# Other orders of the products in a projection block, in the experts and in the second MLP

## The chip, the cores and the metric

The kernel runs on one core of one Trainium2 chip, in one launch, and its time is the device time of that core in microseconds (us). Five engines work side by side, each through its own list of instructions: PE (TensorE, matmuls, with its weight loads shown apart as PEld), DVE (VectorE), ACT (ScalarE), POOL (GpSimd) and SP (SyncE, which here only issues DMAs). They meet through semaphores.

## The reference

Two transformer blocks are applied to 256 tokens of 1024 features. The first block (`first_block`) is a gated branch mixer, cross attention to 256 memory tokens and a two-level mixture of experts; the second (`second_block`) runs two layers with an adaLN modulation each: sparse attention with an MLP, then differential attention with an MLP. Cut to what the change touches:

```python
proj = h @ w_in                                   # 1024 -> 6 widths, and 3 gates of 1024
...
return merged @ w_o
...
k, v = jnp.split(mem_n @ w_xkv, 2, axis=-1)       # mem_n: the memory behind its own norm
...
act = silu(einsum('nd,edf->nef', t, w_e_gate)) * einsum('nd,edf->nef', t, w_e_up)
out = einsum('nef,efd->nd', act * gate, w_e_down) # 16 experts of 256 features
```

All of it is fp32. The sums over the inner dimension may be taken in any order.

## The kernel before

**Three products for one.** Each fp32 operand is split into a high and a low part (`whi`, `wlo` for weights; `hTh`, `hTl` and the like for activations), and a product is high·high + high·low + low·high. Weights come by DMA into `raw`, 512 KB at a time; ACT copies them to `whi` (line L98) and DVE subtracts for `wlo` (L99). `raw`, `whi` and `wlo` have six buffers each. PE then multiplies: `mm_fm` (L140 to L142) with the weights as the stationary operand and 256 tokens as the moving one, `mm_tm` (L147 to L149) with 128 tokens stationary and 512 weight columns moving.

**Blocks.** `fm_block` makes 256 output features in one bank of PSUM, 128 features (f = 0, 1) in each half of it. With an inner dimension of 1024 there are 8 row blocks k, so 2·8·3 = 48 matmuls. A block whose input is still being made (`first=True`, and `out_first`) goes over k outside and f inside; every other block takes f outside and k inside, three products for each. The mixer's `proj`, the keys of the memory (`fm<-memT`), the heads of the cross attention, the output projections (`out_proj`), the gates and the upper halves of both MLPs (`fm<-hT`) are such blocks.

**The memory's path.** `norm_rows` normalises the memory's two tiles of 128 tokens: squares on ACT (L247), then `rv`, `r` (L253, an Exp) and `memx` on DVE (L257). `to_fm` turns them on PE (L338, sixteen transposes in four groups, `ax`), copies them to `memTh` on ACT (L341) and takes `memTl` on DVE (L342). Around it ACT has a sine and a cosine (L591, L592) and two kinds of sigmoids (L637 for the conv branch, `sg`; L642 for the condition, `sgc`), each of which needs another function table than the Exp; a load of a table is `ACT_TABLE_LOAD`. DVE makes the condition (`cond`, L643) from `sgc`.

**Experts.** Each of the 16 experts, four to a group (gi), takes `gu` (8 k by 3 products), then `py` = hidden · w_e_down: for k, for the two halves n, three products, into two banks of PSUM. Behind a group's fourth expert its two banks are split to `yh` (L215, ACT) and `yl` (L216, DVE), and `po` (L1080) sums the group into the residual. Behind the last group come the sums of squares (`ss`, L1092 and L1126) of the next norm.

**The second MLP.** `down` (`mo`, `mm_fm`) goes over k, f and three products, into the halves of four banks.

**Who sets the order.** The program text is not the order of the instructions. A scheduler of the framework simulates the engines and puts each engine's list in the order in which its simulation would start the instructions; dependences and a few fences (`behind`) are all that the text fixes.

Of the kernel before, what the change touches and what calls it, by code (L numbers as in the profile page):

```python
# [19 lines left out]
P = 128  # L20
S = 256
# [17 lines left out]
def two_blocks_kernel(ctx, tc, A, out):  # L39
# [10 lines left out]
    # PSUM's eight banks, shared out anew for each phase: outputs of long runs of matmuls (mm), what hangs  # L50
    # on a chain of other engines (ax), long accumulations (acc), modulation rows (ada)
# [24 lines left out]
    # ---------------------------------------------------------------- helpers  # L76
# [28 lines left out]
    class wmat:  # L105
        """the hi and lo parts of w2d[:, c0:c0+cols], as [128, cols] pairs, one for each 128 rows"""
# [30 lines left out]
    def mm_fm(ps, w, x, xk, c, first, last, ncol=P, **kw):  # L137
        """ps[ncol features, tokens] += w[:, c:c+ncol]^T x[:, xk, :]"""
# [5 lines left out]
    def mm_tm(ps, xT, xk, t0, w, first, last):  # L144
        """ps[128 tokens, cols] += x[:, xk, t0:t0+128]^T w"""
# [4 lines left out]

    def fm_block(w2d, K, c0, x, w=None, first=False):
# [16 lines left out]
    def tm_steps(w2d, c0, xT, emit, cols=512, w=None):  # L168
        """512 output columns for both token tiles, a tile at a time"""
# [33 lines left out]
    def skewed(gens, fill=None):  # L203
        """software pipeline: each round starts a generator and moves the others on by one step, newest first"""
# [20 lines left out]
    def inv_rms(ss, n, scale, tag, pool=None):  # L225
        """1/sqrt(ss * scale + EPS) for ss [128, n], with one Newton step on top of the tables' exp(-ln / 2)"""
# [5 lines left out]
    def newton(ss, y, h, t, scale, add=EPS, p=P):  # L232
        """y = 1/sqrt(ss * scale + add)"""
# [7 lines left out]
    def norm_rows(x, dst):  # L241
        """dst = x / rms(x), for x [128 tokens, 1024]"""
# [20 lines left out]
    def rstd(ss, add=EPS):  # L263
        """1/rms of the tokens from their sums of squares on all partitions"""
# [4 lines left out]
    class norm:  # L269
        """the norm of x times gA plus gB, as hi and lo"""  # L270
# [6 lines left out]
        def squares(self, c):  # L277
            """features 256c on of x: their squares' sums over partitions; those of the first 768 are added up before"""
# [39 lines left out]
    def resid(c, ps, gate=None, nx=None):  # L318
        """features 256c on: x += gate * ps, and what the next norm takes from them"""
# [11 lines left out]
    def to_fm(h, aT, t, g):  # L331
        """rows [128 tokens, 1024] times gains to hi/lo feature-major columns of token tile t"""
# [12 lines left out]
    def out_first(aT, w, k1, k0=0, ps=None):  # L345
        """the first block of out_proj up to row block k1, for an input that is still under way"""
# [7 lines left out]
    def out_proj(aT, w2d, nx, gate=None, ws=(), ps0=None):  # L354
        """x += gate * (a @ w)"""
# [9 lines left out]
    # ---------------------------------------------------------------- constants  # L365
# [10 lines left out]
    # the residual stream, feature-major  # L376
# [7 lines left out]
    # causal mask of a diagonal block, twice  # L384
# [6 lines left out]
    # ---------------------------------------------------------------- adaLN rows  # L391
# [3 lines left out]
    def cols(n, name, *parts):  # L395
        """vectors as columns: rows of 128 values turned, [128, n]"""
# [14 lines left out]
    # a part of a layer's modulation row at a time, 1024 columns, in steps of 128 rows of w_ada: on TensorE, 256 for  # L411
    # each of its four column tiles, or summed up over steps on VectorE
# [22 lines left out]
    def ada_mm(n=1, pool=None):  # L435
        """steps on TensorE, or with a pool for the sum on VectorE"""
# [47 lines left out]
    def adaln(i, j, g):  # L484
        """columns of (1 + scale) * g and shift of sublayer j"""
# [10 lines left out]
    # ================================================================ block 1  # L496
    with tc.tile_pool(name="kv", bufs=1, reuse_waits="tile") as kvp:
# [15 lines left out]
        # ---- gated branch mixer  # L513
        win = A["w_in"][0]
        log_exp()
        with tc.tile_pool(name="mix", bufs=1, reuse_waits="tile") as mx:
# [17 lines left out]
            def turned(src, name, c):  # L534
                """features 256c on of two tiles of rows, feature-major"""
# [18 lines left out]
            # the memory's norm, for its keys and values  # L554
# [10 lines left out]
            # rope tables, [128 tokens, tile, 8]  # L565
# [48 lines left out]
            # conv branch  # L614
# [30 lines left out]
            # gated short conv branch  # L645
# [20 lines left out]
            # pool branch  # L666
# [20 lines left out]
            # layer norm over the conv channels  # L687
# [29 lines left out]
            # gates 1 and 2 with their branches  # L717
# [114 lines left out]
            # logits, feature-major, then turned  # L832
# [11 lines left out]
    # ---- hierarchical mixture of experts  # L844
# [7 lines left out]
    def head_rstd(pool, src, n, dim, tag):  # L852
        """1/rms over the last axis of src [128, n, dim]"""
# [6 lines left out]
    def head_norm(pool, dst, src, n, gain, tag):  # L860
        """dst [128, n, 64] = rms_norm(src) * gain, for src in PSUM"""
# [4 lines left out]
    def rope(pool, dst, src, t, n):  # L866
        """the first 16 of 64 columns of dst [128, n, 64] rotated; dst may be src"""
# [834 lines left out]
```

## Time and profile before

| | before |
|---|---|
| median of three runs | 1259.2 us (1256.54 to 1259.34) |
| span of the profiled execution | 1263.1 us |
| PE busy | 1214.8 us, 96% |
| DVE busy | 891.7 us, 71% |
| ACT busy | 695.9 us, 55% |
| mean granted TensorE clock | 0.974 |
| read from HBM | 255.15 MB |

The profile is one execution of its own, whose span is the time from its first to its last instruction; it is 0.3% longer than the median. "Busy" is the time in which an engine has at least one instruction under way. A matmul's end is modelled, so the pace of a dense stretch is read from the distance between starts. The granted clock is a share of 2.4 GHz.

### The profile page before, as it was taken

The page shows a single profiled execution, that of the slowest core. Times are in us where ns is not written, and L with a number is a line of the kernel's source. Part 1 is how long each engine was busy: PE and PEld are TensorE (multiplying, and loading weights), DVE is VectorE, ACT ScalarE, POOL GpSimd, SP SyncE. Part 2 cuts the span into 40 slices and gives each one's busy share as a digit, 9 for nine tenths or more (in the row PEclk, how much of TensorE's full clock was granted, in tenths as well). Part 3 has the DMA queues.
Part 4 walks back from the last instruction along what each step waited for, and adds up shares of the span by engine and source line. Part 5 has one row for each costly group of instructions (what it writes and reads, how often), then busy time and mean ns, then how long its engine had stood idle before and what let it go on. Part 6 is the DMA issues. An engine that isn't in the chain of part 4 may idle for free.

```text
span 1263.1 us, 22514 instructions
## 1 busy us (share of the span) xinstructions
PE 1214.8 (96%) x8762; PEld 1079.8 (85%) x8762; DVE 891.7 (71%) x1672; ACT 695.9 (55%) x1163; POOL 26.0 (2%) x33
## 2 busy tenths in 40 slices
PE   7999999999879999899999989999999999999998
PEld 6989999989667888688656879999988767999998
DVE  7999967564568999696756685486679766645453
ACT  6644447453357777566346465455556554655453
POOL 0000000000000000060000000000000000000000
PEclk8999999999889999999769999999999999999999
DMA  7565565791267999665431697586746445555551
GB/s 247 190 220 174 159 205 186 269 305 37 97 219 259 347 354 345 231 205 169 149 110 58 213 345 267 192 302 221 281 167 207 130 134 201 196 196 179 194 172 34
DMA packets 177551, 257.76 MB, mean 204 GB/s; under 512 B 14239, under 2 KB 138999, under 8 KB 177436
## 3 DMA queue, kind: packets, MB, share of 16 engines
q1 hardware_dynamic: 177436, 256.24, 61.1%
q8 instruction: 71, 1.16, 0.4%
q14 instruction: 44, 0.36, 0.1%
HBM read 255.15 MB, written 1.05 MB: 203 GB/s over the span
## 4 chain that ended last, share of the span: by engine, by line
PE 65%; DVE 3%; DMA 2%; ACT 1%; issue 1%; ACTq 0%; DVEq 0%
PE fm L141 6%; PE fm L142 6%; PE fm L140 6%; PE mo L140 5%; PE mo L141 5%; PE mo L142 5%; PE tm L147 3%; PE tm L149 3%; PE tm L148 3%; PE gu L149 2%; PE gu L147 2%; PE gu L148 2%; PE s L1393 2%; PE ada L432 1%; PE py L148 1%; PE py L149 1%
## 5 line engine op out<-in xcount | busy, mean ns | idle before, releaser
L99 DVE TENSOR_TENSOR wlo<-raw,whi 128x1024 fp32r<-128x1024 f32 (+1 forms) x382 | 456.8, 1218 | 178.0 <-ACT whi L98 173.9
L98 ACT ACTIVATE whi<-raw 128x1024 fp32r<-128x1024 f32 (+1 forms) x382 | 391.6, 1048 | 275.4 <-PE fm L141 149.3
L141 PE MATMUL fm<-hTl,whi 128*128 128x256 f32 (+1 forms) x968 | 276.7, 286 | 5.6 <-DVE hTl L216 3.9
L140 PE MATMUL fm<-hTh,whi 128*128 128x256 f32 (+1 forms) x968 | 276.3, 286 | 3.2 <-ACT hTh L215 3.2
L142 PE MATMUL fm<-hTh,wlo 128*128 128x256 f32 (+1 forms) x968 | 275.0, 284 | 0.0
L141 PEld LDWEIGHTS fm<-hTl,whi 128*128 128x128 f32 (+1 forms) x968 | 185.8, 192 | 7.7 <-DVE hTl L216 5.8
L140 PEld LDWEIGHTS fm<-hTh,whi 128*128 128x128 f32 (+1 forms) x968 | 185.8, 192 | 5.7 <-ACT hTh L215 4.6
L142 PEld LDWEIGHTS fm<-hTh,wlo 128*128 128x128 f32 (+1 forms) x968 | 185.7, 192 | 0.2
L141 PE MATMUL mo<-ul,whi 128*128 128x256 f32 x512 | 142.8, 280 | 0.0
L142 PE MATMUL mo<-uh,wlo 128*128 128x256 f32 x512 | 142.7, 280 | 0.0
L140 PE MATMUL mo<-uh,whi 128*128 128x256 f32 x512 | 141.7, 281 | 0.0
L141 PEld LDWEIGHTS mo<-ul,whi 128*128 128x128 f32 x512 | 96.3, 188 | 0.0
L142 PEld LDWEIGHTS mo<-uh,wlo 128*128 128x128 f32 x512 | 96.2, 188 | 0.0
L140 PEld LDWEIGHTS mo<-uh,whi 128*128 128x128 f32 x512 | 95.5, 188 | 0.4 <-issue 0.4
L147 PE MATMUL tm<-whi,hTh 128*128 128x512 f32 x176 | 69.4, 400 | 0.7 <-ACT hTh L215 0.7
L148 PE MATMUL tm<-wlo,hTh 128*128 128x512 f32 x176 | 68.9, 393 | 0.0
L149 PE MATMUL tm<-whi,hTl 128*128 128x512 f32 x176 | 68.1, 392 | 0.0
L141 PE MATMUL fm<-oTl,whi 128*128 128x256 f32 x192 | 55.0, 289 | 0.9 <-DVE oTl L1613 0.8
L140 PE MATMUL fm<-oTh,whi 128*128 128x256 f32 x192 | 53.9, 288 | 1.4 <-ACT oTh L1612 1.3
L142 PE MATMUL fm<-oTh,wlo 128*128 128x256 f32 x192 | 53.6, 283 | 0.0
L147 PE MATMUL gu<-whi,xgh 128*128 128x512 f32 x128 | 51.1, 401 | 1.8 <-ACT xgh L1011 1.8
L627 DVE SCALAR_TENSOR_TENSOR acv<-apad,chv,acv 128x256 f32<-128x256 f32 x120 | 51.3, 475 | 0.0
(522 smaller groups left out, 2163.1 us busy)
## 6 DMA issues: line engine op xcount, KB each, us to landing
ada<-in_w_ada_dram SPq DMA_DIRECT2D x96, 512.0 KB, 4.7
raw<-in_w_mlp_in_dram SPq DMA_DIRECT2D x64, 512.0 KB, 3.8
raw<-in_w_mlp_out_dram SPq DMA_DIRECT2D x64, 512.0 KB, 5.1
raw<-in_w_in_dram SPq DMA_DIRECT2D x48, 512.0 KB, 3.8
raw<-in_w_e_down_dram SPq DMA_DIRECT2D x32, 512.0 KB, 5.2
raw<-in_w_e_gate_dram SPq DMA_DIRECT2D x61, 256.0 KB, 5.0
raw<-in_w_e_up_dram SPq DMA_DIRECT2D x61, 256.0 KB
raw<-in_diff_w_in_dram SPq DMA_DIRECT2D x24, 512.0 KB, 4.1
```

The lines of the kernel that those rows point to most:

```text
L98: behind("A", SC.activation(hi[:, :n], raw[:, :n], AF.Copy))
L99: last["lo"] = behind("V", V.tensor_tensor(lo[:, :n], raw[:, :n], hi[:, :n].bitcast(F32), op=OP.subtract))
L140: T.matmul(ps, whi[:, c:c + ncol], xh[:, xk, :], start=first, stop=False, **kw)
L141: T.matmul(ps, whi[:, c:c + ncol], xl[:, xk, :], start=False, stop=False, **kw)
L142: return T.matmul(ps, wlo[:, c:c + ncol], xh[:, xk, :], start=False, stop=last, **kw)
L147: T.matmul(ps, xh[:, xk, t0:t0 + P], w[0], start=first, stop=False)
L148: T.matmul(ps, xh[:, xk, t0:t0 + P], w[1], start=False, stop=False)
L149: return T.matmul(ps, xl[:, xk, t0:t0 + P], w[0], start=False, stop=last)
L432: behind("T", T.matmul(ada_part["ps"][32 * j:32 * j + 32, :], w, r[:, S * j:S * j + S], start=start, stop=stop, skip_group_check=True))
L627: V.scalar_tensor_tensor(acv[:, f, :], apad[:, f, j:j + S], chv[:, f, j:j + 1], acv[:, f, :], op0=OP.mult, op1=OP.add)
L1393: T.matmul(ss[hp][:, :n], u, k[:, gi, 0:t + 1].rearrange("p a s q -> p (a s q)"), start=k is kTd, stop=False)
```

## The change

Every block of `fm_block` but the first ones now takes one of five orders, by turns of a counter. `by_rows` has k outside, then f, then the three products. `by_parts` has k, then the product, then f, so that the half written changes with each matmul. `by_features` has f, k and the products as high·low, high·high, low·high. `by_rows_turned` is `by_parts` with the two halves swapped in the middle product. `by_runs` has f, then the product, then k. Odd experts, and the lower products of the groups 2 and 3, use `mm_tm2`, which takes the low part of the tokens first and the low part of the weights last; the pairs (k, n) of `py` come in two other sequences. In the second MLP (i = 1) `down` has k, product, f. No product is added or removed, and no DMA, tile or buffer is changed; comments are taken out, which moves the line numbers.

```diff
+    def by_rows(ps, w, x, K):
+        for k in range(K):
+            for f in range(2):
+                fence["T"] = mm_fm(ps[:, f * S:(f + 1) * S], w[k], x, k, f * P, k + f == 0, k + f == K,
+                                   skip_group_check=True)
...
+    def by_parts(ps, w, x, K):
+        for k in range(K):
+            for j in range(3):
+                for f in range(2):
+                    a, b = parts(w, x, k, f)[j]
+                    fence["T"] = T.matmul(ps[:, f * S:(f + 1) * S], a, b, start=k + j + f == 0, stop=k + j + f == K + 2,
+                                          skip_group_check=True)
...
+    orders = (by_rows, by_parts, by_features, by_rows_turned, by_runs)
...
-            for f in range(2):
-                for k in range(K):
-                    fence["T"] = mm_fm(ps[:, f * S:(f + 1) * S], w[k], x, k, f * P, k == 0, k == K - 1)
+            orders[turn["fm"] % len(orders)](ps, w, x, K)
+            turn["fm"] += 1
...
+    def mm_tm2(ps, xT, xk, t0, w, first, last):
+
+        xh, xl = xT
+        T.matmul(ps, xl[:, xk, t0:t0 + P], w[0], start=first, stop=False)
+        T.matmul(ps, xh[:, xk, t0:t0 + P], w[0], start=False, stop=False)
+        return T.matmul(ps, xh[:, xk, t0:t0 + P], w[1], start=False, stop=last)
...
-                            for f in range(2):
-                                # one group for the bank: its first product clears both halves
+                            for n, f in ((n, f) for n in range(3) for f in range(2)) if i == 1 else ():
+                                a, b = parts([tuple(v[:, 2 * c * P:] for v in wk) for wk in (w[0], w[1])], u, k, f)[n]
+                                T.matmul(po[c][:, f * S:(f + 1) * S], a, b, start=j + k + n + f == 0,
+                                         stop=j + k + n + f == 19, skip_group_check=True)
```

The scheduler places the other engines' work anew around the new order of the products. Two places show it. The first is the memory's path, 28 to 53 us into the run. On ACT, before, both `r` stand together, then the sine's table, the cosine, the sigmoid's table and the condition's sigmoid:

```order
L253 ACTIVATE r_265<-rv_256 128x1
L253 ACTIVATE r_309<-rv_300 128x1
L591 ACT_TABLE_LOAD
L591 ACTIVATE sin_367<-ang_351 128x16
L592 ACTIVATE cos_368<-kk_360 128x16
L642 ACT_TABLE_LOAD
L642 ACTIVATE sgc_1107<-col0_117 128x8
L98 ACTIVATE whi_645<-raw_643 128x1024
L98 ACTIVATE whi_651<-raw_649 128x1024
L637 ACTIVATE sg_499<-fm_450 128x512
L341 ACTIVATE memTh_251<-ax_271,gcols_249 128x128
```

The same place of ACT now (`whi_645` stands two rows above the first, and `whi_721` and `memTh_251` follow the last):

```order
L305 ACTIVATE r_265<-rv_256 128x1
L98 ACTIVATE whi_651<-raw_649 128x1024
L689 ACT_TABLE_LOAD
L689 ACTIVATE sg_499<-fm_450 128x512
L305 ACT_TABLE_LOAD
L305 ACTIVATE r_309<-rv_300 128x1
L643 ACT_TABLE_LOAD
L643 ACTIVATE sin_367<-ang_351 128x16
L644 ACTIVATE cos_368<-kk_360 128x16
L694 ACT_TABLE_LOAD
L694 ACTIVATE sgc_1107<-col0_117 128x8
L98 ACTIVATE whi_715<-raw_713 128x1024
```

The conv branch's sigmoid and a weight copy now stand between the two `r`, there are two table loads more, and two weight copies more come ahead of `memTh`. On PE, before, the first twelve transposes of the memory stand in the third `proj` block (`fm_518`), at matmul 149 of the program:

```order
L141 MATMUL fm_518<-hTl_166,whi_514 128x256
L142 MATMUL fm_518<-hTh_165,wlo_515 128x256
L338 MATMUL ax_271<-ident_78,memx_253 128x128 x4
L338 MATMUL ax_284<-ident_78,memx_253 128x128 x4
L338 MATMUL ax_315<-ident_78,memx_297 128x128 x4
L140 MATMUL fm_518<-hTh_165,whi_514 128x256
L141 MATMUL fm_518<-hTl_166,whi_514 128x256
```

Now they stand in the fourth (`fm_583`, by `by_rows_turned`), from matmul 190 on:

```order
L170 MATMUL fm_583<-hTl_166,whi_573 128x256 x2
L170 MATMUL fm_583<-hTh_165,wlo_574 128x256
L390 MATMUL ax_271<-ident_78,memx_253 128x128 x4
L390 MATMUL ax_284<-ident_78,memx_253 128x128 x4
L170 MATMUL fm_583<-hTh_165,wlo_574 128x256
L170 MATMUL fm_583<-hTh_165,whi_573 128x256
L390 MATMUL ax_315<-ident_78,memx_297 128x128 x4
L170 MATMUL fm_583<-hTh_165,whi_573 128x256
```

They moved 41 matmuls later. The last four transposes (`ax_328`, row blocks 4 to 7 of the second token tile) moved from matmul 228, ahead of the first product with the memory (248), to 282, behind 43 of these products (from 239 on). The low part of row block 7 (`memTl`) is first used at matmul 371 instead of 314, that of row block 6 at 348 instead of 305.

The second place is the end of the expert layer. On PE, before, the last expert's `py` ends with both halves side by side, n = 0 (`py_7325`) two matmuls ahead of n = 1 (`py_7326`):

```order
L147 MATMUL py_7325<-whi_7491,eah_7455 128x512
L147 MATMUL py_7326<-whi_7491,eah_7455 128x512
L148 MATMUL py_7325<-wlo_7492,eah_7455 128x512
L149 MATMUL py_7325<-whi_7491,eal_7456 128x512
L148 MATMUL py_7326<-wlo_7492,eah_7455 128x512
L149 MATMUL py_7326<-whi_7491,eal_7456 128x512
L1080 MATMUL po_7513<-PT_5938,yh_7507 128x256
```

Now n = 0 ends last:

```order
L200 MATMUL py_7326<-whi_7491,eal_7456 128x512
L201 MATMUL py_7326<-whi_7491,eah_7455 128x512
L200 MATMUL py_7325<-whi_7491,eal_7456 128x512
L201 MATMUL py_7325<-whi_7491,eah_7455 128x512
L202 MATMUL py_7326<-wlo_7492,eah_7455 128x512
L202 MATMUL py_7325<-wlo_7492,eah_7455 128x512
L1135 MATMUL po_7513<-PT_5938,yh_7507 128x256
```

On ACT, before, the two halves of `yh` stand together, ahead of a weight copy for the next layer:

```order
L98 ACTIVATE whi_7558<-raw_7556 128x1024
L215 ACTIVATE yh_7507<-py_7325 128x512
L215 ACTIVATE yh_7507<-py_7326 128x512
L98 ACTIVATE whi_7564<-raw_7562 128x1024
L1089 ACTIVATE sq_7519<-xT_88 128x512 x4
```

Now the copy stands between them, and n = 0, which the first `po` reads, comes second:

```order
L98 ACTIVATE whi_7558<-raw_7556 128x1024
L267 ACTIVATE yh_7507<-py_7326 128x512
L98 ACTIVATE whi_7564<-raw_7562 128x1024
L267 ACTIVATE yh_7507<-py_7325 128x512
L1144 ACTIVATE sq_7519<-xT_88 128x512 x4
```

DVE follows: `wlo_7565` (L99) now stands between the two halves of `yl`. On PE all eight sums of squares of the next norm stand behind the last `po`, where two of them stood between the third and the fourth before.

## Rows read from the trace of the kernel before

**Rows 1.** The page, busy time and instructions of each engine.

```profile
PE 1214.8 (96%) x8762; PEld 1079.8 (85%) x8762; DVE 891.7 (71%) x1672; ACT 695.9 (55%) x1163; POOL 26.0 (2%) x33
```

**Rows 2.** The first stretch of 100 us: length, busy us of PE, PEld, DVE, ACT, POOL; PEclk, DMA, GB/s.

```profile
0.00:100.00 100.00, 89.41 (x618) 83.61 (x619) 88.92 (x208) 57.17 (x97) 1.28 (x11) 0.97 0.68 219
```

**Rows 3.** Idle time of PE by what ended it: total us, times, longest.

```profile
PE ax L338 <- issue: 1.8, 1, 1.8
```

**Rows 4.** Starts on PE in dense stretches: start us, us, engine, line, operation.

```profile
718.75 0.28 PE L140 MATMUL fm<-oTh,whi 128*128 128x256 f32 x1
...
719.35 0.28 PE L142 MATMUL fm<-oTh,wlo 128*128 128x256 f32 x1
...
1178.07 0.28 PE L142 MATMUL mo<-uh,wlo 128*128 128x256 f32 x1
...
1179.01 0.28 PE L141 MATMUL mo<-ul,whi 128*128 128x256 f32 x1
```

**Rows 5.** Groups by shape on PE: us busy, mean ns of one | idle.

```profile
L148 PE MATMUL gu<-wlo,xgh 128*128 128x512 f32 x128 | 50.8, 398 | 0.0
...
L148 PE MATMUL py<-wlo,eah 128*128 128x512 f32 x64 | 25.6, 405 | 0.5 <-DVE wlo L99 0.5
```

**Rows 6.** ACT in order of time, 28 to 35 us.

```profile
27.93 1.06 ACT L98 ACTIVATE whi<-raw 128x1024 fp32r<-128x1024 f32 x1 [0.99 <-PE fm L141]
...
29.08 0.33 ACT L253 ACTIVATE r<-rv 128x1 f32<-128x1 f32 x2
...
30.84 0.20 ACT L592 ACTIVATE cos<-kk 128x16 f32<-128x16 f32 x1
31.05 1.28 ACT L642 ACT_TABLE_LOAD   x1
32.34 0.21 ACT L642 ACTIVATE sgc<-col 128x8 f32<-128x8 f32 x1
32.46 1.99 ACT L98 ACTIVATE whi<-raw 128x1024 fp32r<-128x1024 f32 x2
...
34.83 0.35 ACT L341 ACTIVATE memTh<-ax,gcols 128x128 fp32r<-128x128 f32 x1
```

**Rows 7.** DVE in order of time, 32 to 57 us.

```profile
32.58 0.17 DVE L643 TENSOR_TENSOR cond<-col,sgc 128x8 f32<-128x8 f32 x1 [2.08 <-ACT sgc L642]
...
32.86 1.68 DVE L257 TENSOR_SCALAR memx<-memx,r 128x512 f32<-128x512 f32 x4
...
52.57 0.34 DVE L342 SCALAR_TENSOR_TENSOR memTl<-ax,gcols,memTh 128x128 fp32r<-128x128 f32 x1
52.83 4.43 DVE L627 SCALAR_TENSOR_TENSOR acv<-apad,chv,acv 128x256 f32<-128x256 f32 x11
```

**Rows 8.** DMA issues, 14 to 50 us: KB each, median us from issue to landing.

```profile
raw<-in_w_xkv_dram SPq DMA_DIRECT2D x12, 512.0 KB, 4.5
```

**Rows 9.** SyncE's DMA issues in order of time, 28 to 47 us.

```profile
28.33 17.16 SPq L92 DMA_DIRECT2D raw<-in_w_xkv_dram  x10
```

**Rows 10.** PE in order of time, 33 to 35 us and 45 us.

```profile
33.45 1.50 PE L338 MATMUL ax<-ident,memx 128*128 128x128 f32 x12 [1.83 <-issue]
...
45.23 0.28 PE L140 MATMUL fm<-memTh,whi 128*128 128x256 f32 x1
```

**Rows 11.** The end of the expert layer: ACT, DVE and PE in order of time.

```profile
523.45 1.09 ACT L215 ACTIVATE yh<-py 128x512 fp32r<-128x512 f32 x2 [3.11 <-PE py L149]
...
524.08 1.29 DVE L216 TENSOR_TENSOR yl<-py,yh 128x512 fp32r<-128x512 f32 x2 [1.53 <-ACT yh L215]
...
526.09 1.22 DVE L99 TENSOR_TENSOR wlo<-raw,whi 128x1024 fp32r<-128x1024 f32 x1
...
524.10 0.51 PE L1080 MATMUL po<-PT,yh 128*128 128x256 f32 x2 [0.22 <-ACT yh L215]
...
531.33 1.89 PE L1126 MATMUL ss<-sq,ones 128*128 128x256 f32 x8
```

**Rows 12.** DVE behind the last block of an output projection.

```profile
1065.27 0.88 DVE L326 SCALAR_TENSOR_TENSOR xT<-fm,modc,xT 128x256 f32<-128x256 f32 x2 [0.87 <-PE fm L142]
```

More of the change, by code (lines that the diff above doesn't have):

```diff
@@ L149, in mm_tm, with parts, by_rows_turned, by_features @@
         return T.matmul(ps, xl[:, xk, t0:t0 + P], w[0], start=False, stop=last)
+    turn = {"fm": 0}
+    def parts(w, x, k, f):
+        (whi, wlo), (xh, xl) = w[k], x
+        return (whi[:, f * P:(f + 1) * P], xh[:, k, :]), (whi[:, f * P:(f + 1) * P], xl[:, k, :]), \
+            (wlo[:, f * P:(f + 1) * P], xh[:, k, :])
+    def by_rows(ps, w, x, K):
[3 more added lines that the diff above has]
+                                   skip_group_check=True)
+    def by_rows_turned(ps, w, x, K):
+        for k in range(K):
+            for j, ff in enumerate(((0, 1), (1, 0), (0, 1))):
+                for f in ff:
+                    a, b = parts(w, x, k, f)[j]
+                    fence["T"] = T.matmul(ps[:, f * S:(f + 1) * S], a, b, start=k + j + f == 0, stop=k + j + f == K + 2,
+                                          skip_group_check=True)
+    def by_parts(ps, w, x, K):
+        for k in range(K):
+            for j in range(3):
+                for f in range(2):
+                    a, b = parts(w, x, k, f)[j]
+                    fence["T"] = T.matmul(ps[:, f * S:(f + 1) * S], a, b, start=k + j + f == 0, stop=k + j + f == K + 2,
+                                          skip_group_check=True)
+    def by_features(ps, w, x, K):
+        for f in range(2):
+            for k in range(K):
+                for j in (1, 0, 2):
+                    a, b = parts(w, x, k, f)[j]
+                    fence["T"] = T.matmul(ps[:, f * S:(f + 1) * S], a, b, start=k == 0 and j == 1, stop=k == K - 1 and j == 2)
+    def by_runs(ps, w, x, K):
+        for f in range(2):
+            for j in range(3):
+                for k in range(K):
+                    a, b = parts(w, x, k, f)[j]
+                    fence["T"] = T.matmul(ps[:, f * S:(f + 1) * S], a, b, start=k == 0 and j == 0, stop=k == K - 1 and j == 2)
+    orders = (by_rows, by_parts, by_features, by_rows_turned, by_runs)
[4 more added lines that the diff above has]
+        return T.matmul(ps, xh[:, xk, t0:t0 + P], w[1], start=False, stop=last)
     def fm_block(w2d, K, c0, x, w=None, first=False):
@@ L1063, in expert @@
                     py[gi] = [bank("py") for _ in range(2)]
-                for k in range(2):
-                    for n in range(2):
+                for k, n in ((0, 0), (1, 0), (0, 1), (1, 1)) if gi < 2 else ((0, 0), (0, 1), (1, 1), (1, 0)):
+                    if gi < 2:
                         mm_tm(py[gi][n], aT, k, 0, tuple(w[:, 512 * n:512 * n + 512] for w in wd[k]),
                               e == 0 and k == 0, e == 3 and k == 1)
+                    else:
+                        mm_tm2(py[gi][n], aT, k, 0, tuple(w[:, 512 * n:512 * n + 512] for w in wd[k]),
+                               e == 0 and k == 0, e == 3 and k == 1)
                 if e < 3:
@@ L1487, in down @@
                         for k in range(2):
-                            for f in range(2):
+                            for n, f in ((n, f) for n in range(3) for f in range(2)) if i == 1 else ():
+                                a, b = parts([tuple(v[:, 2 * c * P:] for v in wk) for wk in (w[0], w[1])], u, k, f)[n]
+                                T.matmul(po[c][:, f * S:(f + 1) * S], a, b, start=j + k + n + f == 0,
+                                         stop=j + k + n + f == 19, skip_group_check=True)
+                            for f in range(2) if i == 0 else ():
                                 mm_fm(po[c][:, f * S:(f + 1) * S], w[k], u, k, (2 * c + f) * P, j + k + f == 0,
```

2 lines of the change are left out of this document (1 added, 1 removed).

## The prediction

> **What bounds the kernel.** I read the page's busy times first: PE is busy for 1214.8 us, 96% of the span [rows 1], so a change pays only by another number or pace of matmuls or by what is left of PE's idle time, some 48 us in all. Then the first 100 us: PE has only 89.4 of them, with DVE busy for 88.9 [rows 2]. Here PE hangs on the other engines, and a shift of instructions counts. Third, what ended PE's idle time: one wait of 1.8 us at the memory's transposes (L338) [rows 3]. It is 33.45 minus 1.83 us: PE could have begun them at 31.62 [rows 10]. "Issue" as its cause is no more than that the profile found no semaphore for it; DVE's scaling of the memory runs until 34.54, its first half until about 33.7, and the transposes start in it [rows 7].
>
> **The pace of the matmuls.** Number, shapes and DMAs are as before. In a block with f outside, starts 718.75 and 719.35 are five intervals apart: 0.120 us each; in `mo`, where the half changes after three products, 1178.07 and 1179.01 are eight apart: 0.1175 [rows 4]. Within both, neither a repeated stationary operand (high·high, then high·low) nor a new one shows another interval. I take 0 for the pace, and keep both ends. If the new orders reached the pace of `mo`, 80-odd blocks with about 3,870 products would give 3,870 · 0.0025 = 9.7 us back. If writing another half with each matmul costs something, the nearest rows are `py`, which switches between two banks, against `gu`, which stays in one: 405 against 398 ns for one [rows 5], 7 ns on 512 columns. That much on every switching product is the upper end: `by_parts` and `by_rows_turned` have 768 each, the second MLP's `down` 768, so 2,304 · 0.007 = 16 us; in proportion to the columns 8 us. I choose 0 since `py` and `gu` also read other tiles, and `mo` switches halves and is the faster one.
>
> The Trainium skill ("TensorE: Matmul & The Clock Gate", Back-to-back issue gap) gives N/2.4 + 2.5 ns for an isolated matmul, 109 ns for 256 columns, and says that in a stream the weight load takes part too. The trace does not reach 109 ns in either stream above; by that figure alone the moved products would be an estimated 3,870 · 0.011 = 43 us faster, and I give it no weight.
>
> **The memory's path, 28 to 53 us.** I go along ACT as it now stands. `whi_579` ends at 28.99 (27.93 + 1.06) [rows 6]. Then come `whi_645`, `rv` and the first `r`, about 1.5 us, to 30.5. `whi_651` needs its DMA: that is the first of the issues from 28.33 on [rows 9], and such a transfer takes 4.5 us to land in this stretch [rows 8], 32.8 at the latest guess; before, its copy was the second of a pair from 32.46 on that waited for nothing [rows 6]. I take 31.6, between both. From there: the copy 1.0, four tables at 1.28, `sg` 0.5, `r` 0.2, sine and cosine 0.3, `sgc` 0.1: 31.6 + 7.2 = 38.8. DVE's `cond` waits for `sgc`, as it did before at 32.58, and the memory's scaling stands right behind it, 0.84 us for the first tile (half of 1.68) [rows 7]: 39.8. PE would be at the transposes 41 matmuls later than 31.62, at 31.62 + 41 · 0.12 = 36.5. So it waits 3.3 to 3.6 us where it waited 1.8: **+1.7**, from +0.6 (`whi_651` at 30.5) to +2.9 (at 32.8). Queued behind the waiting instructions are, on ACT, `whi_715`, `whi_721` and all of `memTh`; on DVE, `wlo_716`, `wlo_722` and all of `memTl`.
>
> A sentence apart: the Trainium skill ("ScalarE: Activation LUTs", What ACT_TABLE_LOAD costs) has 1,283 ns for the load and 1,380 ns for a drain with it, and its rule is to batch calls by set, which this order breaks. The load here is 1.28 us, but the cosine ends at 31.04, the load starts at 31.05 and `sgc` follows at 32.34 [rows 6]: no drain shows. By the page's total the four tables would add an estimated 5.5 us more; I stay with 1.28.
>
> Second, the products with the memory. Before, the low part of row block 7 was written by 52.57 + 0.34 = 52.9 [rows 7], and PE, which began these products at 45.23 with matmul 248 [rows 10], used it at 314: 45.23 + 66 · 0.12 = 53.2. There was no slack. Now the last four transposes stand at 282. PE is there at about 36.5 + 3.4 + 92 · 0.12 = 50.9, and DVE has between them and the last low part four conv multiplications, thirteen conv steps (4.43 / 11 = 0.4 each [rows 7]), two weight differences (1.22 each [rows 11]) and the low parts (0.3 each), about 11 us: block 6 at about 60, block 7 at 62.5. PE would use them at matmuls 348 and 371, at about 58.8 and 61.6 with the eight short matmuls taken into account. So one more wait of about 1.3 us, from 0 to 3: **+1.3**. Later, the conv chain on DVE and PE are late by about the same, so what hangs on it at 180 to 212 us stays where it was for PE.
>
> **The end of the experts.** Before, `yh` ran from 523.45, the first `po` at 524.10, and the last sums at 531.33 [rows 11]. Now n = 0 is split behind n = 1 and a weight copy (1.06), so the first `po` starts at about 525.5 and its low half, behind `wlo_7565` (1.22), at 526.8 instead of about 524.7. PE used to wait for the residual sums between the `po` and can take some of that back, but all eight sums of squares now stand behind `po`, where two stood in a gap. The ends are 0 (all taken back) and 2.3 (both copies on the path); I take 1.0, near the middle. Against it the one wait of 0.5 us of `py` for `wlo` [rows 5], at this last group, shrinks to 0.2, since that product now stands fifth instead of third. **+0.7**, from -0.3 to +2.0.
>
> **The blocks whose end is waited for.** An output projection's last block sets the next norm. One might expect f outside to let the half f = 0 go early; it does not: DVE took both halves back to back 0.87 us behind the last product [rows 12]. So k outside loses nothing: 0. In dense stretches ACT and DVE split weights up to six buffers ahead, and a block that frees a weight tile earlier or later moves only that: 0, within half a microsecond either way for all of them.
>
> **The sum** on the profiled span: 1263.1 + 1.7 + 1.3 + 0.7 = 1266.8, or +3.7. The span lies 3.9 us above the median of the runs, 1259.2; so I forecast 1259.2 + 3.7 = 1262.9 us. Its terms' ends add up to 0.6 + 0 - 0.3 = +0.3 and 2.9 + 3 + 2.0 = +7.9, so the likeliest case's own range is 1259.5 to 1267.1. A measurement of this kernel can tell about 0.3%, 3.8 us, from no change: below 1255.4 is faster, above 1263.0 slower.
>
> **Rivals.**
> - The reshuffled start is hidden: `whi_651` lands early, and PE's wait at the transposes is taken back because the products with the memory now have two more blocks' work between them. For it: PE had idle time to give in 0 to 100 [rows 2]. Against it: DVE is nearly full there and all of it shifts. +0 to +1: 1259.7.
> - The pace improves: k outside and a half that changes often bring `fm` to 0.1175 us. For it: the faster stream is the one whose halves change [rows 4]. Against it: its tiles differ too. 1259.2 + 3.7 - 9.7 = 1253.2.
> - The pace worsens, on the other side of no change for good: a matmul that writes another half than the one before it pays, as `py` beside `gu` [rows 5]. It decides from about 2 ns for each of 2,304. With 3.5 ns: 1259.2 + 3.7 + 8 = 1270.9.
> - The new orders do not stand on the chip, as the scheduler could undo them: the orders printed for PE speak against it.
>
> **Chances.** The forecast 0.57, hidden 0.18, pace better 0.12, pace worse 0.13; the last rival none. Within the forecast's range about half lies above 1263.0, a little below it the rest. Faster: 0.12 and 0.03 of hidden, 0.15. Slower: 0.13 and 0.30 of the forecast, 0.43. Within 0.3%: 0.42. The range for 8 in 10 takes in most of the worse pace and part of the better: 1255 to 1270.
>
> **What would show it.** In the new profile: a wait of 3 to 4 us at the memory's transposes, near 40 us, with the four table loads ahead of it on ACT; a second wait of one or two us at the products with the memory near 60 us; the last sums of the expert layer about 1 us later behind the last `py`; intervals of 0.120 us in every order of block. I am wrong if the idle time of PE in the first 100 us does not grow by some 3 us, or if the interval within a block depends on its order by more than 1 ns.

## The result, and the profile after

The changed kernel takes 1276.15 us (median of 4 runs, 1270.12 to 1276.88); the kernel before, run beside it, 1259.27 us (4 runs, 1256.54 to 1263.77). The ratio is 1.0111, with an interval of 1.007 to 1.0152: slower by far more than the 0.3% that can be told from no change, and above the range that was forecast, which ended at 1270. Two of the ten runs of the third experiment below took 1671 and 1674 us at a granted clock of 0.65 and are left out of its numbers.

The profiled span is 1274.7 us against 1263.1. From the page of the kernel after, the busy times; and by stretches, the first 100 us (columns as in [rows 2]):

```profile
PE 1216.2 (95%) x8762; PEld 1081.6 (85%) x8762; DVE 893.5 (70%) x1672; ACT 697.4 (55%) x1165; POOL 26.1 (2%) x33
```

```profile
0.00:100.00 100.00, 85.57 (x561) 79.44 (x562) 81.13 (x193) 57.66 (x97) 1.28 (x11) 0.93 0.63 200
```

PE has the same 8762 instructions and 1.4 us more busy time than in [rows 1]; ACT has two more, the table loads. Of the first 100 us PE now has 3.8 less than in [rows 2], DVE 7.8 less, and PE's mean granted clock there is 0.93 where it was 0.97. So the time was not lost in the matmuls' number, and something in the start is late. The waits of PE in the kernel after (total us, times, longest):

```profile
PE ax L390 <- issue: 5.4, 1, 5.4
...
PE ax L1061 <- DVE xgl L1064: 2.5, 3, 1.6
PE po L1135 <- ACT yh L267: 1.9, 1, 1.9
...
PE py L147 <- ACT eah L267: 1.7, 2, 1.2
...
PE fm L186 <- DVE wlo L99: 1.1, 2, 0.7
...
PE po L1135 <- DVE yl L268: 0.9, 1, 0.9
```

L390 is the L338 of before: its wait has grown from 1.8 us [rows 3] to 5.4. The others stand in three places, and the same matmuls compared in both traces (the first or last of each named product) say what each place costs in all. **Start:** the first product behind the start (`tm`, 68.3 us before) is 6.9 us late, and the last of that stage at 257 still 6.8. **Gather:** the first `py` (399.4 us) is 8.3 late, the first `po` (428.0) 11.5: 3.2 more, not all of it lost, as told below. **Tail:** the last `py` (523.5) is 11.4 late, the first `cmp` of the next layer (572.6) 14.2: 2.8 more. Behind that the kernel after gets some of it back and ends 11.6 late; why is told with the last experiments.

**The start.** ACT in order of time in the kernel after, answering to [rows 6]:

```profile
33.41 1.06 ACT L98 ACTIVATE whi<-raw 128x1024 fp32r<-128x1024 f32 x1 [2.00 <-DMA raw<-in_w_xkv_dram]
34.49 1.28 ACT L689 ACT_TABLE_LOAD   x1
35.78 0.60 ACT L689 ACTIVATE sg<-fm 128x512 f32<-128x512 f32 x1
36.40 1.28 ACT L305 ACT_TABLE_LOAD   x1
37.69 0.20 ACT L305 ACTIVATE r<-rv 128x1 f32<-128x1 f32 x1
...
40.83 0.21 ACT L694 ACTIVATE sgc<-col 128x8 f32<-128x8 f32 x1
```

The weight copy `whi_651` stands ahead of the memory's scale and waits 2.00 us for its DMA, until 33.41; then come the four table loads, and `sgc` at 40.83. DVE and PE follow it:

```profile
41.07 0.17 DVE L695 TENSOR_TENSOR cond<-col,sgc 128x8 f32<-128x8 f32 x1 [2.92 <-ACT sgc L694]
41.15 0.88 DVE L309 TENSOR_SCALAR memx<-memx,r 128x512 f32<-128x512 f32 x2
```

```profile
41.74 1.94 PE L390 MATMUL ax<-ident,memx 128*128 128x128 f32 x8 [5.42 <-issue]
...
45.82 0.63 PE L170 MATMUL fm<-hTh,whi 128*128 128x256 f32 x2
46.25 0.63 PE L170 MATMUL fm<-hTl,whi 128*128 128x256 f32 x2
...
47.27 0.40 PE L170 MATMUL fm<-hTl,whi 128*128 128x256 f32 x2
47.51 0.28 PE L170 MATMUL fm<-hTh,wlo 128*128 128x256 f32 x1
```

The transposes begin at 41.74, after 5.42 us without work, 3.6 more than in [rows 10]. But that is half of it. Behind the wait a pair of products takes 0.43 us (45.82 to 46.25); from 47.27 on it takes 0.24. The granted clock says why (length, PE busy, PEclk, DMA, GB/s; kernel after):

```profile
35.00:40.00 5.00, 1.31 (x11) 1.00 1.09 354
40.00:47.00 7.00, 5.26 (x25) 0.51 0.37 117
47.00:48.00 1.00, 1.00 (x11) 1.00 0.79 297
```

It was 1.00 (2.4 GHz) until PE had stood still, 0.51, so nearly all of it at the lower level of 1.2 GHz, for the 5.3 us of work after it, and 1.00 again from 47. The 12 transposes and 13 products from 41.74 to 47.04 take 5.3 us here; at full clock, by the transposes of before (1.25 us from 33.45 to 34.70) and 0.12 us a product, they would take about 2.8. That is an estimated 2.5 us lost. Before, with a wait of 1.8 us, the clock stayed at 1.00 from 35 to 50. A wait for `wlo` follows near 60 us (the other of the two in the list above stands at 765 us, outside the start):

```profile
60.39 0.39 PE L186 MATMUL fm<-memTh,wlo 128*128 128x256 f32 x1 [0.74 <-DVE wlo L99]
```

The three make 3.6 + 2.5 + 0.7 = 6.8, against 6.9 measured.

**The gather.** Just ahead of the first `py` PE gathers the experts' tokens (`ax<-Pm`), and these products wait until DVE has copied earlier ones out of PSUM (`xgl`). Before:

```profile
394.99 0.50 PE L1009 MATMUL ax<-Pm,hMh 128*128 128x256 f32 x2 [0.42 <-DVE xgl L1012]
...
396.84 0.50 PE L1009 MATMUL ax<-Pm,hMh 128*128 128x256 f32 x2 [1.11 <-DVE xgl L1012]
```

The kernel after, PE and its clock:

```profile
403.96 0.51 PE L1061 MATMUL ax<-Pm,hMh 128*128 128x256 f32 x2 [1.59 <-DVE xgl L1064]
...
407.76 0.79 PE L147 MATMUL py<-whi,eah 128*128 128x512 f32 x1 [0.47 <-ACT eah L267]
...
458.71 0.50 PE L147 MATMUL py<-whi,eah 128*128 128x512 f32 x1 [1.23 <-ACT eah L267]
```

```profile
400.00:405.00 5.00, 3.41 (x23) 1.00 1.05 384
405.00:410.00 5.00, 4.06 (x15) 0.53 0.57 186
410.00:415.00 5.00, 5.00 (x21) 0.78 0.00 0
```

Here too the half clock comes behind the wait. All waits for `xgl` together have not grown: 2.5 us in both kernels (of which the first trace counts 0.5 at another line, L1054), but more of it comes in one piece. And 1.2 of the 3.2 us are work, not loss: between the first `py` and the first `po` PE now has 52 products of `py` and 10 transposes, where it had 48 and 8. The products of `py` alone in that stretch, before and after (length, busy, times, PEclk):

```profile
399.42:427.94 28.52, 12.14 (x48) 1.00 0.85 288
```

```profile
407.75:439.48 31.73, 15.56 (x52) 0.93 0.73 240
```

In the executions told below that were at 1.00 here the stretch takes 28.5 to 28.6 us with the first list and 29.7 with the second. So some 2 us are the clock's. Behind the first `po` PE then waits once more for `eah` (1.23 us at 458.71, in the last row of PE above), where before it did not.

**The tail.** `po` waits 1.89 us for `yh` and 0.87 for `yl`, where before it waited 0.22 for each ([rows 11] show the first) and 0.5 for the residual sum, which it doesn't wait for now: 1.8 us more. And again the clock is lowered (0.57 from 538 to 542). Before, then after:

```profile
PE po L1080 <- DVE xT L1083: 0.5, 1, 0.5
...
PE po L1080 <- DVE yl L216: 0.2, 1, 0.2
```

```profile
537.14 0.50 PE L1135 MATMUL po<-PT,yh 128*128 128x256 f32 x2 [1.89 <-ACT yh L267]
538.52 0.58 PE L1135 MATMUL po<-PT,yl 128*128 128x256 f32 x1 [0.87 <-DVE yl L268]
```

**The pace.** One output projection of the kernel after shows four orders in a row (start, us):

```profile
718.73 0.28 PE L186 MATMUL fm<-oTh,whi 128*128 128x256 f32 x1
...
719.91 0.28 PE L186 MATMUL fm<-oTh,wlo 128*128 128x256 f32 x1
...
721.84 0.40 PE L170 MATMUL fm<-oTh,whi 128*128 128x256 f32 x2
722.08 0.40 PE L170 MATMUL fm<-oTl,whi 128*128 128x256 f32 x2
...
727.60 1.12 PE L193 MATMUL fm<-oTh,whi 128*128 128x256 f32 x8
728.55 1.12 PE L193 MATMUL fm<-oTl,whi 128*128 128x256 f32 x8
...
733.36 0.28 PE L140 MATMUL fm<-oTh,whi 128*128 128x256 f32 x1
733.48 0.28 PE L141 MATMUL fm<-oTl,whi 128*128 128x256 f32 x1
```

Ten products in 1.18 us (L186), two in 0.24 (L170), eight in 0.95 (L193), one in 0.12 (L140): 0.118 to 0.120 each, whether the half changes with every product or not. The median over the whole trace is 120 ns in each order of `fm`, and 117 in `mo` in the old order and in the new.

### The profile page after: what moved, and what is told of

Same layout as the page of the kernel before. It is cut to its first block, busy times and chain, and to the rows that moved or that the text cites. A ratio compares the mean times of both kernels' runs of the same rounds, so it can differ in the third digit from the quotient of the medians.

```text
span 1274.7 us, 22533 instructions
## 1 busy us (share of the span) xinstructions
PE 1216.2 (95%) x8762; PEld 1081.6 (85%) x8762; DVE 893.5 (70%) x1672; ACT 697.4 (55%) x1165; POOL 26.1 (2%) x33
## 4 chain that ended last, share of the span: by engine, by line
PE 62%; DVE 4%; DMA 2%; ACT 2%; issue 1%; SPq 0%; ACTq 0%; DVEq 0%
PE mo L1545 7%; PE fm L186 4%; PE fm L170 4%; PE fm L193 3%; PE tm L147 3%; PE tm L149 3%; PE tm L148 3%; PE fm L178 3%; PE mo L141 2%; PE mo L142 2%; PE mo L140 2%; PE s L1448 2%; PE ada L484 1%; DMA ada<-in_w_ada_dram 1%; PE fm L141 1%; PE fm L142 1%
## 5 line engine op out<-in xcount | busy, mean ns | idle before, releaser
L99 DVE TENSOR_TENSOR wlo<-raw,whi 128x1024 fp32r<-128x1024 f32 (+1 forms) x382 | 457.8, 1221 | 181.0 <-ACT whi L98 179.1
L141 PE MATMUL fm<-hTl,whi 128*128 128x256 f32 (+1 forms) x248 | 73.1, 295 | 5.8 <-DVE hTl L268 4.0
L140 PE MATMUL fm<-hTh,whi 128*128 128x256 f32 (+1 forms) x248 | 72.1, 291 | 4.2 <-ACT hTh L267 4.2
L142 PE MATMUL fm<-hTh,wlo 128*128 128x256 f32 (+1 forms) x248 | 71.6, 289 | 0.0
L140 PE MATMUL mo<-uh,whi 128*128 128x256 f32 x256 | 71.0, 281 | 0.0
L141 PEld LDWEIGHTS fm<-hTl,whi 128*128 128x128 f32 (+1 forms) x248 | 48.3, 195 | 7.8 <-DVE hTl L268 5.8
L186 PE MATMUL fm<-hTh,wlo 128*128 128x256 f32 x192 | 54.4, 284 | 0.4 <-DVE wlo L99 0.4
L186 PE MATMUL fm<-hTl,whi 128*128 128x256 f32 x192 | 54.5, 284 | 0.0
L186 PE MATMUL fm<-hTh,whi 128*128 128x256 f32 x192 | 54.3, 283 | 0.0
L140 PEld LDWEIGHTS fm<-hTh,whi 128*128 128x128 f32 (+1 forms) x248 | 48.2, 194 | 5.9 <-ACT hTh L267 5.7
L142 PEld LDWEIGHTS fm<-hTh,wlo 128*128 128x128 f32 (+1 forms) x248 | 48.3, 195 | 0.0
L141 PEld LDWEIGHTS mo<-ul,whi 128*128 128x128 f32 x256 | 48.1, 188 | 0.0
```

The costliest lines, as they stand in the source:

```text
L99: last["lo"] = behind("V", V.tensor_tensor(lo[:, :n], raw[:, :n], hi[:, :n].bitcast(F32), op=OP.subtract))
L140: T.matmul(ps, whi[:, c:c + ncol], xh[:, xk, :], start=first, stop=False, **kw)
L141: T.matmul(ps, whi[:, c:c + ncol], xl[:, xk, :], start=False, stop=False, **kw)
L142: return T.matmul(ps, wlo[:, c:c + ncol], xh[:, xk, :], start=False, stop=last, **kw)
L186: fence["T"] = T.matmul(ps[:, f * S:(f + 1) * S], a, b, start=k == 0 and j == 1, stop=k == K - 1 and j == 2)
```

## The experiments

Three theories of the 1.1% were left: the pace (which the trace already spoke against), the start with its half clock, and the experts. Each experiment is told with its profiled delays against the kernel before's first profile, at the same three places. The kernel before took 1261.65 us beside the first four experiments, 1259.90 beside the single repairs of the experts and the moved transposes, and 1261.60 beside the others; each ratio is against the runs beside it.

**One table load fewer ahead of the memory.** The sigmoid `sg` is put behind the memory's scale again, everything else is as in the kernel after:

```diff
-                SC.activation(sg, pg, AF.Sigmoid)
+                behind("M", SC.activation(sg, pg, AF.Sigmoid))
```

> The changed kernel, with one order more for the scheduler: the conv branch's sigmoid stands behind both r of the memory's norm on ACT, so two of the four table loads between 34 and 41 us go (2 x 1.28 us) and the rest stays. Theory (the order of the products costs nothing by itself; the start loses by ACT's chain in front of the memory's scaling, and by the halved clock behind PE's wait): PE's wait at the transposes falls from 5.4 to about 2.6 us, the half-clock stretch of 6 us goes or shortens, the first product of the tm blocks stands about +2 to +4 us against before instead of +6.9; time about 1272. Rival (the new orders are slower by themselves): the start gains the 2.6 us of tables at most and the time stays above 1273.

It took 1273.58 us (4 runs), ratio 1.0112 [1.006, 1.0165]. The wait fell from 5.42 to 2.41 us:

```profile
38.62 2.06 PE L390 MATMUL ax<-ident,memx 128*128 128x128 f32 x12 [2.41 <-issue]
```

`tm` was 2.8 us late instead of 6.9; the clock still fell behind the wait (0.72 from 40 to 45). So ACT's order makes most of the start's loss. The timed runs don't show the gain of some 4 us: their interval is too wide for it, and their median can't decide between theory (1272) and rival (above 1273).

**The first eight blocks in the old order.** The start's order of ACT and PE is then that of before, with 76 blocks in new orders behind it:

```diff
-            orders[turn["fm"] % len(orders)](ps, w, x, K)
+            if turn["fm"] < 8:
+                for f in range(2):
+                    for k in range(K):
+                        fence["T"] = mm_fm(ps[:, f * S:(f + 1) * S], w[k], x, k, f * P, k == 0, k == K - 1)
+            else:
+                orders[turn["fm"] % len(orders)](ps, w, x, K)
```

> The changed kernel, but its first 8 blocks (four of the conv branch, four of the memory's keys) take the old order, f outside; the other 76 blocks, the experts and the second MLP keep the new ones. Theory: the +6.9 us of the first 70 us go to within 1 us, what the experts lose (3 to 5 us) stays; time about 1269. Rival (the orders themselves are slower): 8 of 84 blocks give back a tenth of the loss, time about 1275.

1266.41 us (10 runs), ratio 1.0035 [1.0007, 1.0064]; `tm` is 0.5 us early. The whole loss of the start is gone. Gather (+3.3) and tail (+4.5) are there as in the kernel after (3.2 and 2.8 in its first profile, 3.4 and 4.4 in its second).

**The experts in the old order**, the projections as in the kernel after (`gu` and `py` both):

```diff
-                    (mm_tm2 if E % 2 else mm_tm)(ps, xe, k, s0, wgu[k], k == 0, k == 7)
+                    mm_tm(ps, xe, k, s0, wgu[k], k == 0, k == 7)
...
-                for k, n in ((0, 0), (1, 0), (0, 1), (1, 1)) if gi < 2 else ((0, 0), (0, 1), (1, 1), (1, 0)):
+                for k in range(2):
+                    for n in range(2):
...
-                    else:
-                        mm_tm2(py[gi][n], aT, k, 0, tuple(w[:, 512 * n:512 * n + 512] for w in wd[k]),
-                               e == 0 and k == 0, e == 3 and k == 1)
```

> The changed kernel with the experts' products as before. Theory: the start stays at +6.9 us; between the last Pm product and the end of the experts the loss of 5 us (3 behind a half-clock stretch at 404 to 412 us, 2 at the end) goes; time about 1271. Rival (the half-clock stretch has to do with the later start and not with the experts' order): 3 of these 5 us stay, time about 1274.

1269.4 us (8 runs), ratio 1.0063 [1.0036, 1.0089]. The start is late by 8.1 us, with a wait of 5.8 and its clock at half behind it; the gather adds 0.0 (10.0 at the first `py` and at the first `po`), the tail 0.0 (11.3 and 11.3).

```profile
42.00:48.00 6.00, 5.20 (x25) 0.50 0.26 87
```

**Both together:** the first eight blocks and the experts as before, by the two edits above, so 76 projection blocks and the second MLP in new orders are what is left.

> Both undone: the first 8 blocks and the experts as before; 76 blocks in the five new orders and the second MLP's down in its new order stay. Theory: no loss is left but fractions of a microsecond, time 1259 to 1264. Rival (orders slower by themselves): nine tenths of the loss stay, time about 1274.

1264.50 us (10 runs), ratio 1.0021 [0.9992, 1.0051], half a microsecond above the range expected and some 10 below the rival, and at the places -0.5, 0.0 and 0.0. The new orders as such cost nothing that can be told from no change (at most 0.5%, by the interval); with the unchanged intervals in the trace, the pace theory falls.

**Which edit makes the gather late.** To the first eight blocks only `gu` is put back:

```diff
-                    (mm_tm2 if E % 2 else mm_tm)(ps, xe, k, s0, wgu[k], k == 0, k == 7)
+                    mm_tm(ps, xe, k, s0, wgu[k], k == 0, k == 7)
```

> The kernel with the first 8 blocks old, and of the experts' changes only gu put back (mm_tm in all experts); py keeps its new orders. Theory (the gather loses because the odd experts begin with the low part of the gathered tokens, which DVE makes last, and the clock then halves; the end loses by the order of the two halves of py): the half-clock stretch near 400 us and its 3.3 us go, the loss behind the last py (4.5 us up to the first cmp in the run with 8 old blocks) stays; time about 1263 against 1266.4. Rival (py's orders cause the gather's loss too): 3.3 us stay, time 1266.

1266.22 us (10 runs), ratio 1.006 [1.0039, 1.008]. The gather's loss is gone from the trace (+1.2 at the first `py` and at the first `po`), the tail's 4.2 stays. But the time is the rival's 1266 and not 1263: the profiled execution was the fastest of the ten, and the timed runs show no gain over the second experiment (1.0035). The theory's reason is not shown either: in the changed order every odd expert begins its `gu` with `xgl`, yet in the kernel after no product of an odd expert's `gu` waits for it; the waits stand at `ax`.

**Which edit makes the tail late.** In the last two groups n = 0 ends before n = 1 again, with the first eight blocks as before:

```diff
-  ... else ((0, 0), (0, 1), (1, 1), (1, 0)):
+  ... else ((0, 0), (0, 1), (1, 0), (1, 1)):
```

> The kernel with the first 8 blocks old, gu with its new orders, and the last two groups' py with the low part of the tokens first as in the changed kernel, but n = 0 before n = 1 for both k. ACT then copies both halves of yh together again, and two of the sums of squares stand between the last po again. Theory: the 4.5 us behind the last py go to within 0.5 us, the gather's 3.3 us stay; time about 1262. Rival (the low part first is what costs at the end): the 4.5 us stay.

The tail's loss is gone (0.2 between the last `py` and the first `cmp`), and `po` waits for `yh` 0.5 us. The start is 0.9 late, with a wait of 2.4 us at the transposes and the clock at 1.00 behind it. The gather shows only 1.2 here, the work that moved, with the same waits for `xgl` as in the kernel after but the clock at 1.00 (length, PE busy, PEclk):

```profile
398.00:405.00 7.00, 6.00 (x34) 1.00 0.52 177
```

In the first experiment it is also 1.2 at 1.00. In the three executions with 3.2 to 3.4 the clock fell to between 0.50 and 0.61. Of all the profiles told here it fell at this place in four of six with `gu` in its new orders, and in one of seven with `gu` as before: the new order makes the fall likelier, but does not settle it, and why is open. Yet the kernel took 1275.85 us (7 runs), 1.0091 [1.0054, 1.0128], which neither theory had. The trace puts most of it in another stage, the sparse attention's (from the first to the last product with `kTd`), whose matmuls and orders the change doesn't touch. This stage in the profiles of before (630), of after (643) and of this kernel (633), and of the two repeats told below:

```profile
630.00:693.00 63.00, 61.74 (x398) 0.83 0.28 89
```

```profile
643.00:703.00 60.00, 58.77 (x392) 0.89 0.30 90
```

```profile
633.00:702.00 69.00, 68.72 (x394) 0.75 0.24 77
```

Its length goes with the clock that it is granted, 55 us at 1.00 and 69 at 0.75. All 7 runs of this kernel were long; whether something in it makes the lower clock likelier is open.

**Both of the experts' repairs**, with the first eight blocks (what is left of the change in the experts are `py`'s order of operands in the last two groups and the order of k and n in the first two):

> All three places put back with as little as was found to matter: the first 8 blocks old, gu old, and n = 0 before n = 1 in the last two groups' py; 76 blocks in the new orders, the second MLP's down, py's other sequences and its low part first stay. Theory (three places lose by waits and the halved clock, nothing else does; the run with the end put back but gu new was long by the granted clock of the sparse attention, 0.75 there, and not by its change): outside the sparse attention's s stage the trace stands within 2 us of before, time 1260 to 1265. Rival (putting the end back costs in the sparse attention): its s stage takes 66 us or more again and the time is above 1270.

In the profile the places cost -0.5, 0.0 and 2.2 (PE waits 1.7 us for the residual sum `xT`, where before it waited 0.5), the sparse attention takes 56 us at 1.00, which refutes the rival, and the span is 1259.9 us. The timed runs are 1266.92 us (10 runs, 1258.99 to 1272.69), ratio 1.0042 [1.0013, 1.007], above what was expected. Some microseconds of these runs are not in the one that was profiled, and are not located.

**The transposes moved, a failed attempt.** To take the wait away instead of its cause, the memory's transposes were put behind four blocks of the convolution, in the kernel after and in the one before:

```diff
-                to_fm(m, aM, t, g_mem)
+                ms.append(m)
...
+            fence["P"] = fence["T"]
+            for t in range(2):
+                to_fm(ms[t], aM, t, g_mem, "P")
```

> The changed kernel with the memory's transposes ordered behind the last of the four conv blocks on PE (the text of the transposes moved there, and a fence), so that 49 products that stood behind PE's wait of 5.4 us are done ahead of it; ACT's chain with its four table loads stays. Theory (idle time and the halved clock behind it, not the table loads by themselves, are what is lost): PE's wait at the transposes goes, some of it comes back as a wait for the first memTh and memTl, 2 to 3 us; the start stands at +3 to +5 us instead of +6.9, time about 1273. Rival: ACT's and DVE's chain ends the stretch anyway, +6.9 as before, time 1276.

> The kernel before with the same move of the memory's transposes behind the four conv blocks. Here the wait is 1.8 us and the clock is whole behind it. If the move pays by itself, up to 1.8 us are gained (1257 to 1259); if the products with the memory then wait for memTl, as they had no slack, it is 0 to 3 us slower (1259 to 1263).

1282.4 us (5 runs), 1.0167 [1.0121, 1.0214], and 1280.47 us (4 runs), 1.0162 [1.0116, 1.0209]. Both wait for something else, the row of biases that is loaded there, and for `memTl`; both are far above what either theory had, and they tell nothing of the first question. In the kernel after with the move:

```profile
PE ax L455 <- DMA rows<-in_b_ada_dram: 5.2, 1, 5.2
PE fm L141 <- DVE memTl L394: 5.2, 3, 4.0
```

**Both kernels once more**, unchanged, one execution of each on one chip:

> The kernel before, unchanged, profiled once more. Theory (the length of the sparse attention's s stage follows the clock granted in that one execution): the stage takes anything from 55 to 69 us, at another granted clock than the 0.83 of the first profile, and the rest of the trace stands within 1.5 us of the first. Rival (each kernel has its own clock there): 63 to 64 us at 0.83 again.

> The changed kernel, unchanged, profiled once more. Both theories: PE's wait at the memory's transposes 5.4 us and the halved clock behind it, the halved clock near 404 us, and the later sums behind the experts return, each within 1 us; the s stage 55 to 69 us.

1259.08 us and 1280.16 us. Here the sparse attention ran at 1.00 in both, the kernel before first:

```profile
630.00:685.00 55.00, 53.80 (x403) 1.00 0.33 105
```

```profile
649.00:704.00 55.00, 53.47 (x393) 1.00 0.31 97
```

The three places against the first profile of before cost 7.2, 3.4 and 4.4 us; the tail's is 1.6 more than in the first profile, with the clock at half for 6.8 us instead of 3.4. The two spans, 1257.1 and 1278.1, are 21.0 us apart, of which 15.6 have come by the first `cmp` (16.6 late against 1.0). Most of the rest is in the 60 us between that and the sparse attention (the delay between the two grows from 15.7 to 19.2 there), at a granted clock of 0.89 in the kernel after and 0.94 in the one before. In the first pair of profiles this stage had been 3.3 us shorter in the kernel after, and hid as much of the loss.

## Why the prediction was wrong

**Right.** *The pace, 0*: measured 0, and the rivals on it, better and worse, are refuted. By the Trainium skill's figure for an isolated matmul ("TensorE: Matmul & The Clock Gate", Back-to-back issue gap) the estimate would have been 43 us faster; the trace disagrees, 0.120 us in every order. *The path on ACT and the place of the wait* were those that were forecast: PE was at the transposes at 36.32 (36.5 forecast), four table loads ahead of it, and the rival that the reshuffled start is hidden is refuted. One reading behind "the blocks whose end is waited for" is off, without effect: the 0.87 us of [rows 12] are DVE's idle time; its two instructions start 0.05 us behind the last product (1064.94 + 0.28 to 1065.27), and both halves do come back to back. *The table load at 1.28 without a drain*: the load behind `sg` starts at 36.40 and `r` at 37.69, so 1.29; the Trainium skill's 1.38 us of drain ("ScalarE: Activation LUTs", What ACT_TABLE_LOAD costs) does not show here either.

**Wrong: the wait at the transposes was mis-sized, +1.7 forecast, +3.6 measured.** The step that failed was "I take 31.6, between both": `whi_651` started at 33.41, later even than the latest guess, 32.8, which the forecast had worked out from the issue at 28.33 and 4.5 us. It was issued at about 28.64 and took 4.8. The mean of two ends was taken where the wait for a DMA was known to stand on the path. That is 1.8 us; another 0.5 is that the steps from there to `cond` took 7.7 instead of 7.2; PE then began 0.3 us sooner behind `cond` than reckoned.

**Wrong: a wait was priced at its own length.** Behind the longer wait the clock was halved for 5 us of work, +2.5 us, and nothing in the sum or in a rival stood for it. The wait of 1.8 us that the forecast looked at had 1.00 behind it, but the trace of before shows the half clock behind a longer wait elsewhere, which was not weighed:

```profile
357.19 0.95 PE L1009 MATMUL ax<-Pm,hMh 128*128 128x256 f32 x3 [3.98 <-DVE Pm L997]
```

```profile
357.26:367.50 10.24, 7.98 (x25) 0.50 0.98 307
```

The Trainium skill ("TensorE: Matmul & The Clock Gate", HAM oscillation — how this bites in real kernels) describes such a case, a stream of matmuls that waits for its operands (there for DMAs) and goes on at half the clock. The trace agrees in kind, and shows that it isn't sure to happen: the gather's wait of 1.6 us had 0.53 behind it in the kernel after and 1.00 in the sixth and first experiments told above.

**Wrong in kind: "one more wait" for `memTl`, +1.3.** It did not come: DVE wrote the last two low parts 4 us later than reckoned (by 63.97 and 66.20), but PE reached their first uses 5 us later (64.02 and 66.88). One wait of 0.7 us for `wlo` came in its place.

**Wrong: "0, within half a microsecond either way for all of them".** This covered every block whose operands are ready ahead. The new order of the experts' `gu` was in the change, and what it does to the gather was not weighed: [rows 5] show `gu` in its dense middle, not at the first experts, where PE stands right behind DVE. The list of PE is another there, the wait for `xgl` comes in one piece, and in most executions the clock falls behind it. Cost in the kernel after: some 2 us of the 3.2 to 3.4, by the clock; the rest is work that moved.

**The end of the experts, +0.7 forecast, +2.8 to 4.5 measured.** The mechanism was right (`yh` of n = 0 behind a weight copy). The upper end of 2.3 was the two copies on the path, and the choice "near the middle" assumed that PE could take back half; it took back 0.5 (the wait for the residual sum), so 1.8 stayed, and the clock fell as well, for the other 1.0 to 2.7.

**In all:** the places cost 6.9 to 7.2, 2.0 to 2.2 (without the work that moved) and 2.8 to 4.4, so 12 to 14 us, where 3.7 were forecast, and 5 to 7 of them are the lowered clock, for which the sum had no term. The mean span of the five executions of the kernel after is 14.3 us above that of 52 of the kernel before. What is shown is that undoing each of the three edits takes its loss away at its place in the trace, and in timed runs that the start costs (1.0063 [1.0036, 1.0089] with the experts alone put back) and, barely clear of nothing, the experts (1.0035 [1.0007, 1.0064] with the start alone put back). Not shown in timed runs is the gather's share by itself, nor a version that keeps all the new orders and times like the kernel before; the one that comes nearest (1.0021) keeps the experts and the first eight blocks as they were.

## What to carry to other kernels

An order of products that costs nothing within a dense stretch can cost at the stretch's two ends, where the other engines' work is placed around it anew: look there, for each stage, at which operand the first product needs and which result the next stage waits for. A wait of PE that grows to some microseconds is to be priced with a possible stretch at half the clock behind it, and a DMA on the path at its late end. With one profile of each kernel, compare delays at named products, stage by stage, before believing the difference of two spans.

## What the runs showed of the hardware

The sparse attention's stage, with the same instructions, took 54.6 us at a granted clock of 1.00 and 63.7 at 0.83 in two executions of the same kernel before, and 69.2 at 0.75 in the longest of all. Most of the scatter of this kernel's times is of that kind: over 116 executions of nine of the kernels told here, a span above its kernel's mean goes with a mean clock below it (correlation -0.79), by about 6.9 us for 0.01 of the clock. What decides the clock in that stage is not shown.
